# A hybrid attention block on one core: one DMA transpose per pair, an earlier weight load, and another order for the last products

## The chip, the cores and the metric

The kernel runs on one core of a Trainium2 chip. The metric is the device time of the whole program in microseconds, the median of several runs. Beside those runs one execution was recorded by the hardware profiler, and all views of the profile come from it.

## The reference

For a sequence of 2048 positions of width 1024, the block computes

```python
h = rms_norm(x, norm_gain)
qa, ka, va, qb, kb, vb, ga, gb, mg = split(h @ w_in)
# q and k are RMS-normed per head; all softmaxes have a relative-position bias
ya = banded_attention(qa, ka, va, window 128, 8 query heads on 2 kv heads, sink) * silu(ga)
yb = softmax-weighted sum of three dilated attentions, (window, dilation) =
     (128, 1), (512, 4), (2048, 16), 8 heads each, * silu(gb)
merged = sigmoid(mg_a + b) * (ya @ w_branch_a) + sigmoid(mg_b + b) * (yb @ w_branch_b)
out = x + merged @ w_out
```

## The kernel before, in words

**One order for five engines.** The program is written out by a heap of due times. `at(t, f)` puts a step at time t, `until(t)` runs all steps that are due, and every step appends its instructions to the engines' streams. Between engines semaphores hold, within an engine the order of writing. Time is counted in slots. Due times are constants: `W_STEP` for the weights, `Y_PART` and `Y_MAX` for the finished columns of y, `L_LAST` for the last logits, `KQ_BUFS` and `PT_BUFS` for the number of buffers.

**Units and pairs.** The input projection and both attentions go in 14 units of 8 slots each: two A units (two kv heads' worth of the windowed attention, numbers 0 and 2) and twelve B units (two heads of one dilation). In each slot one pair of subsets, 2 × 128 positions, is projected on TensorE (L697, into the bank pj). Matrices are split into a high and a low f16 part, so each product takes three matmuls. ScalarE, VectorE and GpSimd take q, k and v out of the bank, norm and split them into the tile spl, and `Pair.turn` (L781) transposes spl by DMA into kq. A unit's `Item`s, two heads at 128 queries each, come some slots later: logits on PE (L847, bank s), maxima on DVE (L862), exponentials on ACT, the high part p on ACT (L875) and the low part on DVE (L879), a DMA transpose of p into pt (L885), and the product with v on PE (L896, bank pv).

**Queues.** All these DMAs are issued by SyncE in the order of the program: kq (L787), pt (L885), raw weights (`w_load`, L178, two issues of 384 KB at a time), the columns of y and the gates (L946 yo, L977 ytd). An issue that waits for its data holds everything behind it. The raw weights of a unit have one buffer, wraw, free once the unit before has been split; then come four squares on ACT (`w_square`), a sum on PE, and the split. kq has 6 tiles of six 128 × 128 blocks, and B units keep the first one of each residue class in another ring, kq0.

**y.** `YPart` takes finished parts of y: four 128 × 128 transposes on PE (L960, into the one bank pt), a gating on DVE that reads that bank (L967, yo) and a store. After a chunk's fourth part, `max1` to `max3` find the chunk's maximum: ym on DVE, a matmul of ym with ones on PE into the same bank pt (L189), and six small DVE operations on the sum (L196 to L204).

**The last attention slots and stage two.** The last pair's logits are `L_LAST` slots later than the others; PE fills the wait with projections of the merge gates (`mg_step`, L304). Then the branch and output products go in groups of seven products (a scheme of Strassen's kind). `run(g)` writes products 0 to 4 of a group with one or two late ones of the group before between them, and leaves 5 and 6 for the next group. The products share three banks:

```python
PROD = (("A11", 0), ("S1", 2), ("A12", 1), ("S2", 0), ("S4", 2), ("S3", 0), ("A22", 0))
```

The number is the bank of the product. A product adds onto what its bank holds (L1921 for a branch, L1993 for the output), and after each DVE or ACT reads the bank: for the output `put` (L2000) adds it, scaled, to a tile xr, which is stored (L2003) when both of its parts are in. `Out(7)` is the last group of the kernel.

Of the kernel before, what the change touches and what calls it, by code (L numbers as in the profile page):

```python
# [22 lines left out]
F16 = mybir.dt.float16  # L23
I32 = mybir.dt.int32
AF = mybir.ActivationFunctionType
OP = mybir.AluOpType
# [6 lines left out]
NT = S // 128  # L33
# [35 lines left out]
Y_PART = (-0.02, 0.571, 0.797, 0.981, 1.031)  # L69
GATE = (-0.062, 0.084, 0.255)  # L70
W_STEP = (0.1, 0.6, 1.9, 0.445, 4.186, 0.117, 0.301)
W_MAX = (3.542, 3.596)
G_PREP = (5.907,)
N_PREP = (5.948, 6.756, 7.277)
Y_MAX = (0.02, 0.445, 0.485)
S_AT = ((26, 8), (50.5, 5.5), (56, 5.5), (72.5, 5.5), (78, 5.5), (94.5, 4.5), (99, 4.5), (103.5, 4.5))
F_AT = (4.6, .12, 5.0, .33, .16, 7.4)
G_US = dict(look=.25, late=.12, add=.7, hi=.64, dma=.4, wl=7.0, sq=.82, pow=1.5, wh=.72, lo=.76, th=.82, p1=.73, st=3.0,
# [1 line left out]
SEQ = ((1, 0), (1, 1), (8, 0), (8, 1), (2, 0), (2, 1), (9, 0), (9, 1), (3, 0), (3, 1), (10, 0), (10, 1), (4, 0), (4, 1),  # L80
       (5, 0), (5, 1), (6, 0), (6, 1), (7, 0))
G_T0, G_LD, G_SQ = 5.0, 3.0, 2.0
W_RAW, L_LAST = 14.0, 0.3
STD, W_EARLY, G_TH, G_SI, G_CP, K_AT = 5.2, 24.0, 2.0, 4.0, 1.0, (4, 17)
Y_S = 4.0
Y_1 = (.2, .9, 1.6), (13.0, 14.0, 1.6)
# [12 lines left out]
X_US = dict(look=0.25, land=4.3, next=1.45, late=.12, sq=1.14, st=.17, ln=.2, nw=.75, sc=1.24, tr=.8, hi=.5, lo=.62, gs=2.1, pw=1.3,  # L99
            gh=1.06, gl=1.26, mm=.217, th=.6, gt=.63, us=.83, uh=.75, ul=.82, ag=1.0, tl=1.3)  # L100
XT_BUFS = 14
KQ_BUFS = 6
VT_BUFS = 10
PT_BUFS = 4
N_BIAS_A = 384
# [3 lines left out]
def block_kernel(tc, x, w_units, w_gate, w_mrg, w_out, w_bra, w_brk, gain, qkg, sink, bias_a, bias_b, b_merge, out):  # L109
    nc = tc.nc  # L110
    V = nc.vector
    A = nc.scalar
    G = nc.gpsimd
    T = nc.tensor
# [12 lines left out]
    def ucol():  # L127

        ucount[0] += 1
        return ubuf[:, ucount[0] - 1:ucount[0]]  # L130
# [252 lines left out]
    def at(t, f, *args):  # L383
        seq[0] += 1
        heapq.heappush(heap, (t, seq[0], f, args))

    now = [0.0]

    def until(t):
        while heap and heap[0][0] <= t:  # L390
            now[0], _, f, args = heapq.heappop(heap)
            f(*args)

    def chain(steps):

        steps = sorted(steps, key=lambda e: e[0])
        done = [0]

        def go(k):
            if done[0] < k or steps[k][1](*steps[k][2:]) is False:  # L400
                at(now[0] + .04, go, k)
            else:
                done[0] = k + 1

        for k, e in enumerate(steps):
            at(e[0], go, k)
# [107 lines left out]
    class Order:  # L514
# [17 lines left out]
        def run(self):  # L532
            while self.steps:
                best = {}
                for n, s in self.steps.items():
                    t = self.start(n)
                    if t is not None:
                        best.setdefault(s[0], []).append((t, s[3], n))
                eng, c = min(best.items(), key=lambda e: min(e[1])[0])
                t0 = min(c)[0]  # L540
                t, _, n = min((x for x in c if x[0] <= t0 + (0 if eng == "T" else X_US["look"])), key=lambda x: x[1])
                eng, us, _, _, f, args, _ = self.steps.pop(n)
                self.end[n] = self.free[eng] = t + us
                at(t, f, *args)
# [15 lines left out]
    for t in range(NT):  # L560
        g = groups[t]
# [8 lines left out]
        for h in range(2):  # L570
            k = 2 * t + h
# [15 lines left out]
    steps = {}  # L587
# [36 lines left out]
    wk = main.enter_context(tc.tile_pool(name="wk", bufs=2, reuse_waits="tile"))  # L624
# [55 lines left out]
    class Pair:  # L680
# [98 lines left out]
                G.tensor_copy(sp[:, i, nh:, :, :], sp[:, i, nq:nh, ::-1, :])  # L779

        def turn(self):  # L781
            for i, s in enumerate(self.subsets):
                if self.un.shift and s[1] == 0:
                    kq = wk.tile([128, 6, 128], F16, name="kq0", bufs=3)
                else:
                    kq = wk.tile([128, 6, 128], F16, name="kq", bufs=KQ_BUFS)
                nc.sync.dma_start_transpose(out=kq[:], in_=self.sp[:, i].rearrange("p a b c -> p (a b c)"))  # L787
                self.un.kq[s] = kq


    class Item:
# [143 lines left out]
    class YPart:  # L935
# [12 lines left out]
        def plan(self, t):  # L948
            steps = [(t + d, f) for d, f in zip(Y_PART, (self.load, self.turn, self.gate, self.top, self.store))]
            if self.q == 3 and self.chunk < 2:  # L950
                steps += [(t + Y_PART[3] + d, f) for d, f in zip(Y_MAX, (self.max1, self.max2, self.max3))]
            chain(steps)
# [253 lines left out]
    w_forms(NU + SEQ[0][0], 8 * NU)  # L1206
    for u in range(NU + 1):
        t = 8 * u
        steps = [(t + W_STEP[i], w_load, u + 1, (2 * i, 2 * i + 1)) for i in range(2)]
        for i in range(4):  # L1210
            steps.append((t + W_STEP[2] + W_STEP[3] * i, w_square, u + 1, i))
            if u < NU:
                steps += [(t + W_STEP[4] + W_STEP[3] * i, w_hi, u + 1, i),
                          (t + W_STEP[4] + W_STEP[5] + W_STEP[3] * i, w_lo, u + 1, i)]
        chain(steps + [(t + d, f, u + 1) for d, f in zip(W_MAX, (w_sum, w_pow))])

    for k in range(8):
        u = 3 + k
        t = 8 * u
# [10 lines left out]
    t = 0  # L1230
    while t < NPAIR or heap or any(k >= t for k in fill):
        u, j = divmod(t, 8)
        steps = [(f, args) for f, *args in fill.pop(t, [])]
# [70 lines left out]
    def bank():  # L1304
        return ps_p.tile([128, 512], F32, name="fps")

    (sb, ib), (so, io) = (scales[k] for k in "bo")
    ysg, yig, msc, bnd, i_o = (ucol() for _ in range(5))
# [420 lines left out]
    for k in range(2):  # L1729
        g = LAST - 2 + k  # L1730
# [36 lines left out]
    def y_build(s, k, b, b0=None):  # L1767
        load, sums, hi, lo = y_parts(s, k)
        at(b if b0 is None else b0, load)
        for n in range(4):  # L1770
            at(b + Y_S + .4 * n, sums, n)
        for n in range(7):
            at(b + Y_S + .9 + .7 * n, hi, n)
            at(b + Y_S + 1.7 + .7 * n, lo, n)
# [25 lines left out]
    ahead = [y_parts(1, k) for k in range(2)]  # L1800
# [14 lines left out]
    class Seven:  # L1815
# [8 lines left out]
        def after(self, i):  # L1824
            b, r = self.b, self.r
            if i == 0:
                self.copy(0, b[0])
            elif i == 1:
                self.copy(2, b[2])
            elif i == 2:  # L1830
                self.sum(0, b[1])
            elif i == 3:
                self.copy(1, b[0])
            elif i == 4:
                self.sum(1, b[2])
            elif i == 5:
                self.sum(2, b[0])
            else:
                self.last(b[0])
# [16 lines left out]
    def emit(g, i):  # L1856
        until(pos[0])
        mm = g.mm(i)
        us = g.mm_us
        for k, m in enumerate(mm):  # L1860
            until(pos[0] + us * k / len(mm))
            m()
        pos[0] += us
        until(pos[0])
        now[0] = pos[0]
        g.after(i)

    pending = []

    def late():  # L1870
        if pending:
            emit(*pending.pop(0))

    def run(g):
        emit(g, 0)
        if g.n == 1:
            late()
            return
        emit(g, 1)
        late()  # L1880
        emit(g, 2)
        emit(g, 3)
        late()
        emit(g, 4)
        pending.extend(((g, 5), (g, 6)))

    def flush():
        while pending:
            pos[0] += .3
            late()  # L1890
# [5 lines left out]
    WO = rp.tile([128, 7, 2, 4, 512], F16, name="WO")  # L1896
# [78 lines left out]
    class Out(Seven):  # L1975
# [11 lines left out]
        def matmuls(self, i, ps, fresh):  # L1987
            m = mf[self.s, i]
            out = []
            for p in range(4):  # L1990
                for ml, wl in ((0, 0), (0, 1), (1, 0)):
                    k = len(out)
                    out.append(lambda p=p, ml=ml, wl=wl, k=k: T.matmul(  # L1993
                        ps[:], lhsT=m[:, ml, p, :], rhs=WO[:, i, wl, p, :],
                        start=(fresh and k == 0), stop=(k == 11), skip_group_check=True))
            return out

        def put(self, h, n, b, store=False):
            t = self.x[h, n]
            at(now[0] + .2, lambda: V.scalar_tensor_tensor(t[:], b[:], i_o[:], t[:], OP.mult, OP.add))  # L2000
            if store:
                t0 = 128 * self.s + 1024 * h
                at(now[0] + 1.0, lambda: nc.sync.dma_start(  # L2003
                    out=out[t0:t0 + 128, 512 * n:512 * n + 512], in_=t[:]))

        def after(self, i):
            b = self.b
            for h, n, k, store in (((0, 0, 0, False),), ((1, 1, 2, False),), ((0, 0, 1, True),), ((0, 1, 0, False),),
                                   ((0, 1, 2, True),), ((1, 1, 0, True),), ((1, 0, 0, True),))[i]:
                self.put(h, n, b[k], store)  # L2010
# [3 lines left out]
    outs = [Out(s) for s in range(8)]  # L2014

    def AB(s):
        p = pos[0]
        at(p + (4.0 if s else 1.0), g_tiles, s, 1)
        if s == 0:
            at(p + 9, g_tiles, 1, 0)  # L2020
            for i in range(7):
                at(p + WO_AT[0] + WO_AT[1] * i, wo_load, i)
        run(Branch(s, 0))
        run(Branch(s, 1))

    AB(0)
    at(pos[0] + 9, outs[0].load, ((0, 0), (1, 1), (0, 1), (1, 0)))
    AB(1)
    for s in range(8):
        p = pos[0]  # L2030
        if s < 6:
            at(p + .1, g_tiles, s + 2, 0)
            y_build(s + 2, 0, p + 5.0, p + .05)
            y_build(s + 2, 1, p + 14.0)
        if s < 7:
            at(p + (24.0 if s < 6 else 2.0), outs[s + 1].load, ((0, 0), (1, 1)))
            at(p + (31.0 if s < 6 else 15.5), outs[s + 1].load, ((0, 1),))
            at(p + (31.1 if s < 6 else 28.0), outs[s + 1].load, ((1, 0),))
        if s == 6:
            flush()  # L2040
        run(outs[s])
        if s < 6:
            AB(s + 2)
    flush()
# [78 lines left out]
```

## Time and profile before

| | us |
|---|---|
| median of 3 runs | 1914.71 |
| the runs | 1913.5 to 1917.62 |
| the profiled execution, its own time | 1916.55 |
| span of its instructions | 1914.3 |
| PE busy | 1873.9 (98%) |
| DVE busy | 1500.7 (78%) |
| ACT busy | 1250.4 (65%) |
| transposes by DMA of spl into kq | 224 issues |
| transposes by DMA of p into pt | 256 issues |

Times in the views run from the start of the span. A wait is put down to what came last by the profile. The DMA share is that of the core's 16 DMA engines, and a value over 1 means that transfers lay over one another.

### The profile page before, as it was taken

To read this page: it belongs to the slowest core of one execution; us is meant where nothing else is said; L and a number is where in the kernel's file an instruction comes from. 1 tells how busy PE (TensorE), PEld (TensorE's weight loads), DVE (VectorE), ACT (ScalarE), POOL (GpSimd) and SP (SyncE) were. 2 spreads that over 40 slices of the span, in tenths; PEclk is the share of its full clock that TensorE was granted. 3 is DMA by queue.
4 is the path that set the end of the run, shared out by engine and by line. 5 is a ranking of instruction groups with operands and counts; after the bars stand their busy time and mean duration, and the time that the engine had idled before them with its cause. 6 is when DMAs were issued, how large, how long until landed. Compare 5 with 4: busy or idle time off the path is not lost.

```text
span 1914.3 us, 51103 instructions
## 1 busy us (share of the span) xinstructions
PE 1873.9 (98%) x19242; PEld 1438.9 (75%) x19242; DVE 1500.7 (78%) x3835; ACT 1250.4 (65%) x3015; POOL 579.0 (30%) x1363
## 2 busy tenths in 40 slices
PE   6999999999999999999999999999999999999998
PEld 4567887889999899998999899544444446776774
DVE  7679878986887879878788888748679644987885
ACT  8577768887676777777776766565666865433431
POOL 1034343443454435534455444300000001322121
PEclk9999999999999999999999999999999999999999
DMA  6259998988889679888897777786666648854541
GB/s 256 83 98 197 164 185 134 192 161 178 149 161 181 134 158 200 151 170 169 143 179 144 147 154 132 165 309 172 211 198 188 190 156 273 290 164 122 148 148 65
DMA packets 639351, 326.21 MB, mean 170 GB/s; under 512 B 459264, under 2 KB 589952, under 8 KB 636672
## 3 DMA queue, kind: packets, MB, share of 16 engines
q1 hardware_dynamic: 638960, 322.70, 73.3%
q8 instruction: 150, 2.46, 0.6%
q14 instruction: 97, 0.79, 0.2%
q10 hardware_dynamic: 144, 0.26, 0.0%
HBM read 139.08 MB, written 73.66 MB: 111 GB/s over the span
## 4 chain that ended last, share of the span: by engine, by line
PE 90%; DMA 5%; DVE 2%; ACT 1%; issue 1%; POOL 0%; SPq 0%; DVEq 0%; POOLq 0%
PE pj L697 43%; PE fps L1602 17%; PE fps L1921 8%; PE fps L1993 8%; PE s L847 5%; PE pv L896 4%; DMA pt<-p 2%; PE pj L352 2%; PE pj L304 1%; PE fps L304 1%; DMA kq<-spl 1%; PE pt L960 1%; DMA bigl<-sd 1%; DVE pr L862 0%; PE s L482 0%
## 5 line engine op out<-in xcount | busy, mean ns | idle before, releaser
L697 PE MATMUL pj<-wl,XH 128*128 128x128 f16 (+2 forms) x2816 | 715.8, 268 | 0.0
L697 PE MATMUL pj<-wh,XL 128*128 128x128 f16 (+2 forms) x2816 | 712.2, 269 | 0.0
L697 PE MATMUL pj<-wh,XH 128*128 128x128 f16 (+2 forms) x2816 | 709.4, 268 | 0.0
L697 PEld LDWEIGHTS <-XH 128*128 128x128 f16 x5632 | 575.3, 112 | 54.5
L697 PEld LDWEIGHTS <-XL 128*128 128x128 f16 x2816 | 315.9, 112 | 24.0
L862 DVE CUSTOM_DVE_ANT_0 pr<-s,b,ubuf 128x256 f32<-128x256 f32 (+3 forms) x512 | 218.9, 465 | 44.1 <-PE s L847 41.7
L879 DVE SCALAR_TENSOR_TENSOR p<-pr,p 128x512 f16<-128x512 f32 (+2 forms) x256 | 195.7, 765 | 51.6 <-ACT p L875 50.4
L764 POOL TENSOR_TENSOR rw<-rw,g 128x128 f32<-128x128 f32 (+1 forms) x224 | 149.1, 686 | 202.5 <-DVE rw L757 183.2
L1931 POOL TENSOR_TENSOR g<-g,t 128x512 f32<-128x512 f32 x32 | 48.8, 1526 | 523.7 <-DVE t L1854 523.7
L1602 PEld LDWEIGHTS <-wh 128*128 128x128 f16 x1064 | 104.1, 99 | 123.5 <-issue 0.4
L715 ACT ACTIVATE rw<-pj 128x256 f32<-128x256 f32 (+1 forms) x224 | 87.5, 390 | 134.5 <-PE pj L697 134.0
L779 POOL COPY spl<-spl 128x256 f16<-128x256 f16 (+1 forms) x224 | 96.4, 460 | 246.5 <-DVE spl L774 246.5
L875 ACT ACTIVATE p<-pr 128x512 f16<-128x512 f32 (+2 forms) x256 | 157.7, 616 | 14.4 <-DMA pt<-p 10.1
L1921 PE MATMUL fps<-y,bigh 128*128 128x128 f16 x1792 | 153.5, 219 | 0.8 <-DVE r L1854 0.8
L847 PE MATMUL s<-kq 128*128 128x128 f16 (+1 forms) x1856 | 148.2, 218 | 4.8 <-DMA kq<-spl 3.9
L1921 PE MATMUL fps<-y,bigl 128*128 128x128 f16 x896 | 151.7, 219 | 0.0
L1993 PE MATMUL fps<-WO,mf 128*128 128x512 f16 x672 | 150.3, 379 | 0.8 <-DVE xr L2000 0.8
L847 PEld LDWEIGHTS <-kq 128*128 128x128 f16 x2016 | 131.0, 98 | 21.1 <-issue 5.7
L1921 PEld LDWEIGHTS <-bigh 128*128 128x128 f16 x1792 | 139.0, 98 | 8.2 <-issue 0.9
L896 PE MATMUL pv<-vt,pt 128*128 128x65 f16 (+1 forms) x2784 | 132.1, 193 | 8.7 <-DMA pt<-p 7.7
L896 PEld LDWEIGHTS <-pt 128*128 128x128 f16 x3024 | 119.6, 98 | 24.6 <-DMA pt<-p 12.5
L770 ACT ACTIVATE spl<-rw 128x512 f16<-128x512 f32 (+1 forms) x112 | 72.1, 643 | 79.7 <-POOL vt L726 71.4
(252 smaller groups left out, 3815.0 us busy)
## 6 DMA issues: line engine op xcount, KB each, us to landing
wraw<-in_w_units_dram SPq DMA_DIRECT2D x56, 384.0 KB, 4.8
g<-mgd SPq DMA_DIRECT2D x64, 256.0 KB, 5.4
wraw<-in_w_mrg_dram SPq DMA_DIRECT2D x45, 256.0 KB, 4.2
mgd<-t SPq DMA_DIRECT2D x43, 256.0 KB, 2.9
zd<-z SPq DMA_DIRECT2D x128, 66.0 KB, 2.0
zz<-zd SPq DMA_DIRECT2D x64, 132.0 KB, 3.5
xt<-in_x_dram SPq DMA_DIRECT2D x16, 512.0 KB, 7.8
ytd<-yo SPq DMA_DIRECT2D x32, 256.0 KB, 3.5
```

What stands on the lines that cost most here:

```text
L697: out.append(lambda lhs=lhs, rhs=rhs, ch=ch, a=a, b=b, k=k: T.matmul(ps[:, a:b], lhsT=lhs[:, ch, :], rhs=rhs[:, ch, a:b], start=(k == 0), ...
L715: A.activation(self.rw[:, n * i:n * i + n], self.ps[i][:, :n], AF.Copy)
L764: G.tensor_tensor(q[:, i, :un.nq, :], q[:, i, :un.nq, :], g, OP.mult)
L779: G.tensor_copy(sp[:, i, nh:, :, :], sp[:, i, nq:nh, ::-1, :])
L847: T.matmul(self.sv[j][:, o:o + k1 - k0], lhsT=q[:, h, :], rhs=kt[:, un.nq + kh + v * un.nk, k0:k1], start=(v == 0), stop=(v == 1))
L862: V.tensor_tensor_reduce(out=self.pv[:, j, self.p0:self.p0 + W], in0=self.sv[j], in1=un.bias[:, self.h0 + j, self.b0:self.b0 + W], scale=I ...
L875: A.activation(self.sp[:, :128 * n], self.pr, AF.Copy, scale=PSC)
L879: V.scalar_tensor_tensor(self.sp[:, 128 * n:], self.pr, PSC, self.sp[:, :128 * n], OP.mult, OP.subtract)
L896: T.matmul(self.po[:, j, :w], lhsT=p[:, n * j + s, :], rhs=un.v[key][:, vh, c0:c0 + w], start=(k == 0 and s == 0), stop=(k == 2 and s == n ...
L1602: T.matmul(b[k][:], lhsT=w[:, i, ch, :], rhs=xform(PROD[i][0], lo, ch, q), start=(i < 3 and n == 0), stop=(n == 11), skip_group_check=True)
L1921: out.append(lambda p=p, c=c, wl=wl, yl=yl, n=n: T.matmul(ps[:, 128 * p:128 * p + 128], lhsT=w[wl][:, i, c, p, :], rhs=y[:, yl, c, :], sta ...
L1993: out.append(lambda p=p, ml=ml, wl=wl, k=k: T.matmul(ps[:], lhsT=m[:, ml, p, :], rhs=WO[:, i, wl, p, :], start=(fresh and k == 0), stop=(k ...
```

## The change

1. `Pair.turn`: in A units one DMA transpose takes both subsets of a pair (twelve blocks); B units still take two, into the halves of one tile. kq has 4 tiles of twelve blocks; kq0 has one, for dilation 1 alone.
2. `W_SOON`: the raw weights of unit 2 are loaded 1.9 slots sooner and squared 0.5 slot sooner.
3. `Y_MAX`: the matmul of ym and the operations on its sum come 0.065 slot sooner.
4. `L_LAST`: the last pair's logits come 0.1 slot later.
5. The last group on each side (`Branch(7, 1)` and `Out(7)`) takes products in the order 0, 1, 3, 2, 5, 4, 6. `Out(7)` makes its last product in two halves of 256 columns. The right half goes into a bank of its own, and VectorE adds it and stores it while the left half runs; the left half follows, and the output's last tile is stored as two pieces of 128 × 256.

```diff
+W_SOON = (1.9, .5)
-Y_MAX = (0.02, 0.445, 0.485)
+Y_MAX = (0.02, 0.38, 0.42)
-W_RAW, L_LAST = 14.0, 0.3
+W_RAW, L_LAST = 14.0, 0.4
-KQ_BUFS = 6
+KQ_BUFS = 4
...
         def turn(self):
+            kq = wk.tile([128, 12, 128], F16, name="kq", bufs=KQ_BUFS)
+            outs = [kq[:, 6 * i:6 * i + 6] for i in range(2)]
+            if self.un.shift and self.un.n == NT and self.subsets[0][1] == 0:
+                outs[0] = wk.tile([128, 6, 128], F16, name="kq0", bufs=1)[:]
+            if self.un.kind == "A":
+                nc.sync.dma_start_transpose(out=kq[:], in_=self.sp[:].rearrange("p s a b c -> p (s a b c)"))
             for i, s in enumerate(self.subsets):
-                if self.un.shift and s[1] == 0:
-                    kq = wk.tile([128, 6, 128], F16, name="kq0", bufs=3)
-                else:
-                    kq = wk.tile([128, 6, 128], F16, name="kq", bufs=KQ_BUFS)
-                nc.sync.dma_start_transpose(out=kq[:], in_=self.sp[:, i].rearrange("p a b c -> p (a b c)"))
-                self.un.kq[s] = kq
+                if self.un.kind == "B":
+                    nc.sync.dma_start_transpose(out=outs[i], in_=self.sp[:, i].rearrange("p a b c -> p (a b c)"))
+                self.un.kq[s] = outs[i]
...
-        steps = [(t + W_STEP[i], w_load, u + 1, (2 * i, 2 * i + 1)) for i in range(2)]
+        ahead = W_SOON if u == 1 else (0.0, 0.0)
+        steps = [(t + W_STEP[i] - ahead[0], w_load, u + 1, (2 * i, 2 * i + 1)) for i in range(2)]
         for i in range(4):
-            steps.append((t + W_STEP[2] + W_STEP[3] * i, w_square, u + 1, i))
+            steps.append((t + W_STEP[2] + W_STEP[3] * i - ahead[1], w_square, u + 1, i))
...
-    def run(g):
+    def run(g, final=False):
...
-        emit(g, 2)
-        emit(g, 3)
+        for i in (3, 2) if final else (2, 3):
+            emit(g, i)
         late()
-        emit(g, 4)
-        pending.extend(((g, 5), (g, 6)))
+        for i in (5, 4) if final else (4,):
+            emit(g, i)
+        pending.extend(((g, 6),) if final else ((g, 5), (g, 6)))
...
         def matmuls(self, i, ps, fresh):
+            if (self.s, i) == (7, 6):
+                fb = bank()
+                for h in range(2):
+                    c, o = slice(256 - 256 * h, 512 - 256 * h), (fb[:, :256], ps[:, :256])[h]
+                    for p in range(4):
+                        for ml, wl in ((0, 0), (0, 1), (1, 0)):
+                            k = len(out)
+                            out.append(lambda p=p, ml=ml, wl=wl, c=c, o=o, h=h, k=k: T.matmul(
+                                o, lhsT=m[:, ml, p, :], rhs=WO[:, i, wl, p, c], start=(k == 0), stop=(k % 12 == 11),
+                                skip_group_check=True))
+                    if h == 0:
+                        out.append(lambda: self.half(1, fb[:, :256]))
+                return out
...
+        def half(self, j, b, store=True):
+            c, t0 = slice(256 * j, 256 * j + 256), 128 * self.s + 1024
+            t = self.x[1, 0]
+            V.scalar_tensor_tensor(t[:, c], b, i_o[:], t[:, c], OP.mult, OP.add)
+            if store:
+                nc.sync.dma_start(out=out[t0:t0 + 128, c], in_=t[:, c])
...
         def after(self, i):
+            if (self.s, i) == (7, 6):
+                self.half(0, b[0][:, :256])
+                return
+            if (self.s, i) == (7, 5):
+                at(now[0] + .4, lambda: self.half(1, b[0][:, 256:], False))
...
-        run(Branch(s, 1))
+        run(Branch(s, 1), s == 7)
...
-        run(outs[s])
+        run(outs[s], s == 7)
```

Two places show how the rows move. SyncE's queue before, in the second half of the first A unit (spl is a pair's normed q and k, p the probabilities of an item, wraw the raw weights, yo a gate's columns):

```order
L885 DMA_TRANSPOSE pt_1762<-p_1722 128x12x128
L787 DMA_TRANSPOSE kq<-spl 128x6x128 x2
L885 DMA_TRANSPOSE pt_1844<-p_1795 128x12x128
L885 DMA_TRANSPOSE pt_1909<-p_1868 128x12x128
L885 DMA_TRANSPOSE pt_1975<-p_1935 128x12x128
L885 DMA_TRANSPOSE pt_2040<-p_2000 128x12x128
L787 DMA_TRANSPOSE kq<-spl 128x6x128 x2
L885 DMA_TRANSPOSE pt_2115<-p_2073 128x12x128
L946 DMA yo<-gtd_87 128x512
L885 DMA_TRANSPOSE pt_2179<-p_2139 128x12x128
L885 DMA_TRANSPOSE pt_2241<-p_2207 128x12x128
L671 DMA b_2297<-in_bias_b_dram 128x512
```

Behind these rows stand, in the same queue before:

```order
L885 DMA_TRANSPOSE pt_2317<-p_2266 128x12x128
L178 DMA wraw<-in_w_units_dram 128x768 x2
L787 DMA_TRANSPOSE kq<-spl 128x6x128 x2
L946 DMA yo<-gtd_88 128x512
L885 DMA_TRANSPOSE pt_2417<-p_2357 128x12x128
```

The same place of the queue now (lines past the change are one to four higher):

```order
L889 DMA_TRANSPOSE pt_1754<-p_1714 128x12x128
L179 DMA wraw<-in_w_units_dram 128x768 x2
L788 DMA_TRANSPOSE kq<-spl 128x12x128
L889 DMA_TRANSPOSE pt_1837<-p_1787 128x12x128
L889 DMA_TRANSPOSE pt_1902<-p_1861 128x12x128
L179 DMA wraw<-in_w_units_dram 128x768 x2
L889 DMA_TRANSPOSE pt_1970<-p_1928 128x12x128
L889 DMA_TRANSPOSE pt_2035<-p_1995 128x12x128
L788 DMA_TRANSPOSE kq<-spl 128x12x128
L889 DMA_TRANSPOSE pt_2108<-p_2068 128x12x128
L950 DMA yo<-gtd_87 128x512
L889 DMA_TRANSPOSE pt_2172<-p_2132 128x12x128
```

Each pair's two kq transposes have become one, and the loads of wraw have moved from ahead of the kq with yo_88 behind it to two kq sooner.

The second place is PE where the first chunk's maximum is summed, in the B unit behind (pj is the projection's bank, ya a finished part of y, ym the maximum). Before, ahead of the eight matmuls of a pair of logits:

```order
L697 MATMUL pj<-wh,XL 128x256
L697 LDWEIGHTS XH
L697 MATMUL pj<-wh,XH 128x256
L697 LDWEIGHTS XH
L697 MATMUL pj<-wl,XH 128x256
L960 MATMUL pt<-idf,ya 128x128 x4
L697 LDWEIGHTS XL
L697 MATMUL pj<-wh,XL 128x256
L847 LDWEIGHTS kq
```

There is no matmul of ym there; it stands some 30 matmuls further on, behind other projections. Now the same place reads:

```order
L698 MATMUL pj<-wh,XL 128x256
L190 MATMUL pt<-ym,ones 128x1
L698 LDWEIGHTS XH
L698 MATMUL pj<-wh,XH 128x256
L698 LDWEIGHTS XH
L698 MATMUL pj<-wl,XH 128x256
L698 LDWEIGHTS XL
L698 MATMUL pj<-wh,XL 128x256
L851 LDWEIGHTS kq
```

The matmul of ym has come ahead of the four transposes, which now stand behind those eight logits and three more projections; both write the bank pt.

## The prediction

> **What bounds the kernel now.** The page comes first: its totals and the chain that ended last.
>
> ```profile
> span 1914.3 us, 51103 instructions
> PE 1873.9 (98%) x19242; PEld 1438.9 (75%) x19242; DVE 1500.7 (78%) x3835; ACT 1250.4 (65%) x3015; POOL 579.0 (30%) x1363
> PE 90%; DMA 5%; DVE 2%; ACT 1%; issue 1%; POOL 0%; SPq 0%; DVEq 0%; POOLq 0%
> ```
>
> TensorE is busy for 98% of the span and is 90% of the chain. The change takes no matmul columns away, so only the idle stretches of PE and its clock can give time. The second view is the windows by stage: first A unit's start, its end, the B unit behind it, and the middle of the second A unit. The last two rows are from a finer cut, over a stretch of 3.5 us and the one behind it.
>
> ```profile
> core 0: us, PE busy (x) PEld busy (x) DVE busy (x) ACT busy (x) POOL busy (x), PEclk, DMA share, GB/s
> 130.00:160.00 30.00, 28.50 (x376) 20.78 (x372) 28.94 (x71) 25.87 (x60) 13.85 (x27) 1.00 0.93 157
> 160.00:205.00 45.00, 40.13 (x617) 36.76 (x615) 39.27 (x99) 34.43 (x78) 14.95 (x35) 0.97 1.11 207
> 205.00:265.00 60.00, 58.09 (x866) 57.50 (x865) 50.49 (x140) 40.63 (x110) 23.54 (x60) 1.00 0.91 161
> 340.00:400.00 60.00, 58.42 (x759) 49.66 (x757) 54.98 (x142) 51.20 (x120) 25.20 (x49) 1.00 1.04 192
> ...
> 201.90:205.40 3.50, 3.50 (x32) 2.84 (x33) 1.97 (x5) 3.13 (x7) 0.00 (x0) 0.51 1.00 216
> 205.40:210.00 4.60, 4.60 (x81) 4.57 (x80) 3.59 (x9) 2.71 (x9) 0.08 (x1) 1.00 0.97 205
> ```
>
> From 160 to 205 PE lacks 4.9 us, the DMA engines have no room (a share of 1.11), and for 3.5 us right behind that the granted clock is 0.51. What PE waited for, from 82 to 265, then from 300 to 400, in the drain of the attention around 1210, and in the last 55 us (line, releaser: total us, times, longest):
>
> ```profile
> PE pv L896 <- DMA pt<-p: 5.5, 5, 2.0
> PE pt L189 <- DVE yo L967: 0.9, 1, 0.9
> ...
> PE pv L896 <- DMA pt<-p: 2.2, 4, 0.7
> ...
> PE s L847 <- DMA kq<-spl: 1.6, 1, 1.6
> ...
> PE fps L1993 <- DVE xr L2000: 0.8, 1, 0.8
> PE fps L1921 <- DVE r L1854: 0.8, 1, 0.8
> ```
>
> These five places, 11.8 us, are what the change touches, and with the clock they bound what it can bring.
>
> **Where the transposes of p wait.** Three of the five products that waited, in the timeline of PE, then the DVE operation that makes the second one's p, and SyncE's queue around its transpose:
>
> ```profile
> 154.21 0.71 PE L896 MATMUL pv<-vt,pt 128*128 128x65 f16 x18 [0.67 <-DMA pt<-p]
> 182.42 0.71 PE L896 MATMUL pv<-vt,pt 128*128 128x65 f16 x18 [1.91 <-DMA pt<-p]
> 201.89 1.15 PE L896 MATMUL pv<-vt,pt 128*128 128x65 f16 x18 [2.03 <-DMA pt<-p]
> ...
> 171.40 0.96 DVE L879 SCALAR_TENSOR_TENSOR p<-pr,p 128x768 f16<-128x768 f32 x1 [0.19 <-ACT p L875]
> ...
> 171.44 1.41 SPq L178 DMA_DIRECT2D wraw<-in_w_units_dram  x2
> 172.94 2.67 SPq L787 DMA_TRANSPOSE kq<-spl  x2
> 175.66 0.57 SPq L946 DMA_DIRECT2D yo<-gtd  x1
> 176.34 1.43 SPq L885 DMA_TRANSPOSE pt<-p  x1
> ...
> L885 SPq DMA_TRANSPOSE pt<-p x13: 1425/2530/3185, 156.8 to 200.1; - x13
> DMA to landing us min/median/max: 3.7/5.0/6.7
> ...
> L787 SPq DMA_TRANSPOSE kq<-spl x28: 1209/1239/2356, 99.1 to 259.3; - x28
> ...
> L178 SPq DMA_DIRECT2D wraw<-in_w_units_dram x4: 423/500/924, 171.4 to 182.5; - x4
> ```
>
> p is there at 172.36 (171.40 + 0.96), its transpose is issued only at 176.34: SP has in between two loads of raw weights, two transposes of kq and a load of yo to issue. So 4.0 us pass before the issue and 6.0 behind it (to 182.4), where the quickest of the thirteen landed after 3.7.
>
> **Part 1, one transpose of 12 blocks for a pair.** Only A units change, 16 of 112 pairs. Two issues of 1.239 (the median) become one; the nearest rows of a 12-block transpose are those of pt, whose issue takes 1.425 at best and 3.185 at worst. Per pair SP then gains 2.48 − 1.43 = 1.05 us or loses 0.71. I take the gain at the places where the queue is late only because SP is, since those waits lie after a stretch of issues without pause. The bytes stay the same, so DMA time is left alone. What the 6-block form hid was that its first half could land sooner; the matmuls of L847 need the second subset as well, so nothing waits for a half alone.
>
> **Part 2, the second A unit's raw weights 1.9 slots sooner.** Two pairs of loads leave the places ahead of the kq at 172.94 (1.41 us of SP there) and, a little later, ahead of another pt. By the order they go two kq sooner: one pair of loads ahead of a kq, the other between the second and third of the four transposes of p behind it. There SP had slack:
>
> ```profile
> SPq L885 <- DVE p L879: 4.7, 4, 1.7
> ```
>
> This is the queue's own wait from 136 to 158: 4.7 us in which SP stood ready for p. Four loads at the 0.5 us of the row above go into that, and DMA share there was 0.93 against 1.11 later. The squares come half a slot sooner on ACT, the same four operations, ahead of ACT's exps; ACT is at 25.87 of 30 there, so I cost them at nothing, with one exp (the wait of 1.7 above as the most) as the price if that cover is gone.
>
> Together, parts 1 and 2 take 1.05 + 1.41 = 2.46 us of the 4.0 before the issue at 176.34, and take the load's DMA traffic out of the crowded window. Of the five waits (5.5 us) four lie there or behind, 4.8 us; the one that ends at 154.2 lies where the loads now go, and I keep its 0.7. Of the four I keep 1.8, some 0.45 each, since DVE (39.27 of 45 busy) would make p late in part: 4.8 − 1.8 = **3.0** us, with bounds of 0 and 5.5. The window at 0.51 lasts 3.5 us and does 1.75 us of work at full clock: **1.7** us come back if the wait of 2.03 that ends at 201.89, where the slow stretch begins, is gone.
>
> On that clock the row says that a wait of 2.0 us, in 11.9 us with 9.5 busy, was followed by the slow stretch. [...]
>
> In the second A unit part 1 acts alone (its weights went with the first). Four waits, 2.2 us, the longest 0.7, each shorter than the 1.05 that SP gains per pair; but DVE is at 54.98 of 60, so p itself is late at some: **1.3** of 2.2, bounds 0 and 2.2.
>
> **Part 3, y's maximum.** ym stood ready long before the bank was free, and PE's first matmul of L189 waited for L967 to read the bank that four transposes had filled:
>
> ```profile
> 252.88 0.16 DVE L983 TENSOR_TENSOR ym<-ym 128x1 f32<-128x1 f32 x1
> ...
> 257.97 0.67 DVE yo L967
> 258.63 0.14 issue
> 258.77 0.35 PE pt L189 x2
> ```
>
> ym is made at 253.04. Put ahead of the transposes at 255.2, that matmul finds an empty bank. What is late next is the transposes, which must wait until DVE's L196 has read the sum; they stand eight logits and more matmuls behind it in the new order, a microsecond or more. I take **0.9**, bounds 0 and 0.9; a wait of the transposes as long as the old one is the lower bound.
>
> **Part 4, last logits 0.1 slot later.** Three matmuls of the filling (L304) move ahead of them.
>
> ```profile
> 1204.86 5.25 DMA kq<-spl
> ...
> 1226.33 2.59 PE pj L304 x12
> ```
>
> 2.59 / 12 = 0.216 each, so 3 × 0.216 = **0.65** of the 1.6 that PE stands until the kq lands at 1210.1 is filled. The work behind it moves by as much later, but PE has only filling matmuls to do there. Bounds 0 and 1.6.
>
> **Part 5, the last products.** Two products in a row on one bank wait until DVE has read it: 0.8 (L1993) and 0.8 (L1921), both named above; in the new order another bank's product of 2.6 us stands between, against 0.75 us of DVE.
>
> ```profile
> 1907.87 2.75 PE L1993 MATMUL fps<-WO,mf 128*128 128x512 f16 x12 [0.84 <-DVE xr L2000]
> 1910.65 0.75 DVE L2000 SCALAR_TENSOR_TENSOR xr<-fps,ubuf,xr 128x512 f32<-128x512 f32 x1 [2.84 <-PE fps L1993]
> ...
> 249.97 0.55 PE pj L697 x5
> ...
> L1763 DVE SCALAR_TENSOR_TENSOR y<-tq,ubuf,y 128x256 f16<-128x256 f32 x60 | 28.8, 483 | 2.9 <-ACT y L1759 2.9
> ```
>
> The last product becomes 24 matmuls of 256 columns; five of that width took 0.55, so 24 take 2.64 against 2.75: no loss. The DVE operation that closes it is 0.75 at 512 wide and 0.48 at 256 (the row with f16 out), 0.3 less, and the other half's work lies beside the matmuls. 0.8 + 0.8 + 0.3 = **1.9**, bounds 1 and 2.
>
> **The sum.** 3.0 + 1.7 + 0.9 + 1.3 + 0.65 + 1.9 = 9.45 us. The profiled execution took 1916.55 (span 1914.3 and 2.25 around it), 1.84 above the median of three runs, 1914.71 (1913.5 to 1917.62). From the median: 1914.71 − 9.45 = **1905.3**.
>
> **The rivals.**
>
> *All of it goes.* The transposes' waits vanish whole in both A units, the clock stays up, and the drain's wait too: 5.5 + 1.7 + 0.9 + 2.2 + 1.6 + 1.9 = 13.8, which gives 1900.9. For it: SP's lateness explains most of the 4.0 us. Against it: DVE and the DMA share.
>
> *Another engine holds the A units.* If p, or the DMA engines at 1.11 with unchanged bytes, sets the pace, the transposes land as late as now and only parts 3, 4 and 5 count: 0.9 + 0.65 + 1.9 = 3.45, or 1911.3. For it: 54.98 of 60 on DVE; against it: p was ready 4.0 us ahead of its issue.
>
> [...]
>
> *Slower: the big transpose holds the queue.* A 12-block transpose behind another is held for up to 3.185 us in the rows above. If each merged kq is, the following pt is issued 3.185 − 2.48 = 0.71 later than now; over 16 pairs 11.3 us. Parts 3 to 5 still give 3.45: 1914.71 + 11.3 − 3.45 = 1922.6. It decides where the pt behind a kq is issued more than 3.4 us after that kq (176.34 − 172.94 now). Against it: the yo and two waits of the ring lie in that 3.4 already, and only nine of the pairs have PE waiting.
>
> That the change doesn't do what it says holds in part: transposes per pair reach only the A units, so the 96 pairs of B units give nothing; that is in the sum.
>
> **How the numbers follow.** The forecast has 0.45, the full recovery 0.20, the A units held otherwise 0.16, the clock 0.09, the slower case 0.10. The range reaches from a little under the full recovery, 1899, to a little over the third case, 1912, and leaves out the slower case and the edges. About 0.2%, 3.8 us, is what a measurement here can tell from no change, as the three runs lie 4.1 apart. Forecast, full recovery and clock are faster by more: 0.74. The third case is a gain of 3.45, within it: 0.16. Slower: 0.10.
>
> **What would show it.** Right: between 160 and 205 PE's waits for pt near 2.5 us, a granted clock of 1.00 around 202, the pt behind a merged kq issued under 3 us after it; no wait of L189's matmul for L967; the drain's wait for kq near 1.0; no wait for xr or r in the last 50 us. Wrong: an issue of the merged kq near 3 us, a wait for pt around 152 to 160 longer than 0.7, or squares that push exps back there.

## The result and the profile after

The changed kernel takes 1908.05 us in the median of 6 runs (1906.96 to 1910.0) against 1915.3 before (6 runs of the same kind, 1913.5 to 1918.9). The ratio is 0.996, 95% interval 0.9947 to 0.9973: faster by 7.25 us, where the prediction had 9.45. The profiled execution took 1910.0 us, 2.0 above its median, and its span is 1908.0.

The page of the changed kernel, for the rows shown of before:

```profile
span 1908.0 us, 51104 instructions
PE 1873.8 (98%) x19254; PEld 1441.1 (76%) x19254; DVE 1501.3 (79%) x3837; ACT 1250.6 (66%) x3015; POOL 581.7 (30%) x1363
```

PE's busy time is what it was (1873.9 before), so the gain is idle time that has gone. Its windows, with the same cuts, and in the last two rows a finer cut:

```profile
core 0: us, PE busy (x) PEld busy (x) DVE busy (x) ACT busy (x) POOL busy (x), PEclk, DMA share, GB/s
130.00:160.00 30.00, 26.70 (x357) 19.58 (x355) 27.86 (x69) 24.43 (x57) 11.95 (x24) 1.00 0.98 185
160.00:205.00 45.00, 43.04 (x649) 39.95 (x648) 40.22 (x101) 36.55 (x84) 17.55 (x38) 0.96 1.09 189
205.00:265.00 60.00, 59.41 (x883) 59.07 (x881) 52.38 (x152) 41.42 (x108) 24.89 (x62) 1.00 0.96 165
340.00:400.00 60.00, 59.00 (x759) 50.70 (x758) 55.28 (x142) 52.45 (x125) 25.97 (x52) 1.00 1.05 196
...
178.00:184.60 6.60, 4.69 (x67) 4.33 (x64) 6.46 (x18) 3.04 (x6) 3.39 (x4) 1.00 1.19 187
184.60:188.10 3.50, 3.49 (x42) 3.31 (x43) 3.22 (x7) 3.05 (x7) 1.24 (x2) 0.55 1.07 235
```

From 160 to 205 PE is busy for 2.9 us more, but from 130 to 160 for 1.8 less: it was 28.50 there before. The stretch at half clock is still there, at another place: 0.55 over 3.5 us, as 0.51 over 3.5 us before. What PE waited for now, from 82 to 265 (three rows), from 300 to 400, and from 400 to 1195 (where before had 2.3 us in 2 waits):

```profile
PE pv L900 <- DMA pt<-p: 3.6, 3, 1.9
PE s L851 <- DMA kq<-spl: 1.5, 1, 1.5
PE s L851 <- DVE nmA L866: 0.7, 2, 0.5
...
PE pv L900 <- DMA pt<-p: 0.9, 2, 0.6
...
PE s L851 <- DMA kq<-spl: 2.7, 3, 1.1
```

The wait of L189 for L967 (0.9), the drain's wait for kq (1.6) and both of 0.8 at the end have no row any more, nor has the wait of 2.03 at 201.89. A wait for kq that was not there before has come to the first A unit. In the timeline of PE it stands at 153.87:

```profile
153.87 0.61 PE L851 MATMUL s<-kq 128*128 128x128 f16 x8 [1.46 <-DMA kq<-spl]
156.08 0.71 PE L900 MATMUL pv<-vt,pt 128*128 128x65 f16 x18 [1.12 <-DMA pt<-p]
184.61 0.89 PE L900 MATMUL pv<-vt,pt 128*128 128x65 f16 x18 [1.92 <-DMA pt<-p]
```

SyncE's queue of the changed kernel just before the first two of them, and how long that kq took from its issue to landing:

```profile
145.69 1.37 SPq L179 DMA_DIRECT2D wraw<-in_w_units_dram  x2
147.10 2.58 SPq L788 DMA_TRANSPOSE kq<-spl  x1
149.86 5.54 SPq L889 DMA_TRANSPOSE pt<-p  x2
...
DMA to landing us min/median/max: 6.7/6.7/6.7
```

Before, the same pair's two transposes were issued at 145.7 and 147.3 and landed like this:

```profile
L787 SPq DMA_TRANSPOSE kq<-spl x2: 1278/1446/1613, 145.7 to 147.3; - x2
DMA to landing us min/median/max: 2.8/3.0/3.1
```

The issue came no later than the second of these two; it is the landing that took 6.7 us instead of 3. Two things have changed there, the size of the transpose and the two loads of 384 KB ahead of it. Part 1 alone, one of the experiments below, has the merged transpose at this place with no load ahead:

```profile
L787 SPq DMA_TRANSPOSE kq<-spl x1: 1808/1808/1808, 145.7 to 145.7; - x1
DMA to landing us min/median/max: 4.3/4.3/4.3
```

So 1.3 us of the difference go with the size and 2.4 with the loads.

### The profile page after: what moved, and what is told of

It is laid out like the page before. It is cut to its first block, busy times and chain, and to the rows that moved or that the text cites. A ratio compares the mean times of both kernels' runs of the same rounds, so it can differ in the third digit from the quotient of the medians.

```text
span 1908.0 us, 51104 instructions
## 1 busy us (share of the span) xinstructions
PE 1873.8 (98%) x19254; PEld 1441.1 (76%) x19254; DVE 1501.3 (79%) x3837; ACT 1250.6 (66%) x3015; POOL 581.7 (30%) x1363
## 3 DMA queue, kind: packets, MB, share of 16 engines
q8 instruction: 150, 2.46, 0.6%
## 4 chain that ended last, share of the span: by engine, by line
PE 89%; DMA 6%; DVE 2%; ACT 1%; issue 1%; POOL 0%; SPq 0%; DVEq 0%; POOLq 0%
PE pj L698 42%; PE fps L1607 18%; PE fps L1927 8%; PE fps L2012 7%; PE s L851 5%; PE pv L900 4%; DMA kq<-spl 2%; DMA pt<-p 2%; PE pj L353 2%; PE pj L305 1%; PE fps L305 1%; PE pt L964 1%; DMA bigl<-sd 1%; PE s L483 0%; DVE pr L866 0%
## 5 line engine op out<-in xcount | busy, mean ns | idle before, releaser
L851 PE MATMUL s<-kq 128*128 128x128 f16 (+1 forms) x1984 | 152.2, 217 | 5.7 <-DMA kq<-spl 4.2
```

The source lines that it names most:

```text
L851: T.matmul(self.sv[j][:, o:o + k1 - k0], lhsT=q[:, h, :], rhs=kt[:, un.nq + kh + v * un.nk, k0:k1], start=(v == 0), stop=(v == 1))
```

## The experiments

Five parts are told apart: 1, one transpose per pair; 2, the raw weights sooner; 3, y's maximum; 4, the last logits; 5, the last products. Each kernel was timed in five rounds beside the kernel before; ratios are to it.

**Parts 1 and 2 alone, 1 alone, 2 alone, and the other three.** The edits, each on the kernel before:

```diff
 parts 1 and 2:  + turn() with one 12-block transpose in A units, + W_SOON = (1.9, .5)
 part 1:         + turn() with one 12-block transpose in A units (with its ring, KQ_BUFS = 4)
 part 2:         + W_SOON = (1.9, .5)
 parts 3 to 5:   + Y_MAX = (0.02, 0.38, 0.42), + L_LAST = 0.4, + run(g, final), half()
```

> Parts 1 and 2 alone (one 12-block kq transpose per pair in A units, raw weights of unit 2 sooner). Theory of the queue: both parts relieve SyncE in the A units, 1.3 us in the second and 1.7 in the first, so about 3 us less than before, ratio 0.9984; the first A unit keeps waits of about 3.6 us for pt, 1.5 for kq, and its stretch at half clock. Rival (the loads only move a wait): the same total here, but all of it from part 1, which the next two kernels tell.

> Part 1 alone. Theory of the queue: 1.3 us less in the second A unit and about 1 in the first, 2.3 in all, ratio 0.9988; the wait for kq at 154 that the changed kernel has is absent, since no load stands ahead of that kq. Rival (the loads only move a wait): about 3 us less, all that parts 1 and 2 bring.

> Part 2 alone. Theory of the queue: 1 to 2 us less, ratio 0.9993; waits for pt between 180 and 203 fall from 4.9 us to under 3, and a new wait of 1 to 1.5 us stands near 154, for kq or pt. Rival (the loads only move a wait): within 0.5 us of before; what goes from 180 to 203 comes back near 154.

> Parts 3, 4 and 5 alone (y's maximum, last logits, last products). By the waits that are gone in the changed kernel's profile, 0.9 + 1.5 + 1.9 = 4.3 us less than before, ratio 0.9978; by the terms of the prediction, with 0.65 for the last logits, 3.45 less. Rival: the drain's wait for kq went because the A units changed, not by the 0.1 slot; then it stands here still with about 1 us.

| kernel | us | ratio, 95% interval |
|---|---|---|
| parts 1 and 2 | 1912.74 | 0.9987 (0.9978 to 0.9996) |
| part 1 | 1910.18 | 0.9976 (0.9967 to 0.9985) |
| part 2 | 1917.83 | 1.0017 (1.0008 to 1.0026) |
| parts 3 to 5 | 1909.1 | 0.9973 (0.9963 to 0.9984) |

The kernel before took 1914.32 here. Part 1 brings 4.1 us, more than either theory had; part 2 does not move a wait at no cost but loses 3.5, and 2.6 on top of part 1. Both theories were wrong on part 2, and parts 1 and 2 together bring 1.6 us where both had 3. The three others bring 5.2; the drain's wait for kq is 0.6 in their profile, so most of it goes without the change in the A units, against the rival. Waits of PE for DMA in part 1 alone, from 82 to 265 and from 300 to 400, and the issues and landings of its sixteen merged transposes:

```profile
PE pv L899 <- DMA pt<-p: 4.2, 3, 1.9
...
PE pv L899 <- DMA pt<-p: 0.2, 1, 0.2
...
L787 SPq DMA_TRANSPOSE kq<-spl x16: 1424/1519/2584, 99.4 to 371.6; - x16
DMA to landing us min/median/max: 3.6/4.2/5.9
```

No wait for kq stands in the A units. The second A unit loses 0.2 instead of 2.2, and one issue of 1.52 takes the place of two of 1.24, 0.96 less. In part 2 alone the same views read:

```profile
PE pv L897 <- DMA pt<-p: 4.3, 5, 1.5
...
PE pv L897 <- DMA pt<-p: 2.8, 5, 0.8
...
154.00 0.71 PE L897 MATMUL pv<-vt,pt 128*128 128x65 f16 x18 [1.48 <-DMA pt<-p]
167.63 0.71 PE L897 MATMUL pv<-vt,pt 128*128 128x65 f16 x18 [0.60 <-DMA pt<-p]
```

As expected of a wait that moves, 1.48 stands at 154 where 0.67 stood, and 0.60 behind it. From 82 to 265 the sum is still 1.2 less than before, so this stretch doesn't show the 3.5 us that the runs lose; and this execution, 1915.23, was 2.6 us under the median of part 2 alone.

**The change without part 2, and its two single parts.**

```diff
 without part 2: - W_SOON = (1.9, .5)
 part 5 alone, on the kernel before: + run(g, final), half()
 part 4 alone, on the kernel before: + L_LAST = 0.4
```

> The change without part 2 (the raw weights of unit 2 at their old place). Part 1 alone gave 4.1 us, parts 3 to 5 gave 5.2, part 2 lost 3.5. If the parts add up, 9.3 us less than before, about 1905.0, ratio 0.9951, and 2 to 3 us less than the changed kernel: part 2 is a loss. Rival (parts 1 and 2 belong together once the rest is in): about the changed kernel's 1907 to 1908.

> Part 5 alone (the last products). By the prediction 1.9 us less than before, ratio 0.9990, both waits of 0.8 gone and the last DVE operation 0.5 instead of 0.75. Parts 3 to 5 together gave 5.2 where the waits sum to 4.3; if the rest of it comes from here, 2.8 less.

> Part 4 alone (the last pair's logits 0.1 slot later). By the prediction 0.65 us less than before and a wait of about 1.0 for kq left there; by the changed kernel's profile, where no such wait is left, 1.5 less; in the profile of parts 3 to 5 a wait of 0.6 was left, which says 1.0 less.

Without part 2 the kernel takes 1904.31, ratio 0.9943 (0.993 to 0.9955), 9.5 us less than before (1913.77 in this group): the parts add up, 4.1 + 5.2 = 9.3, and its median is the lowest of all that ran. Part 5 alone: 1911.67, ratio 0.9987 (0.9979 to 0.9996), 2.1 less. Part 4 alone: 1912.8, ratio 0.9993 (0.9984 to 1.0002), 1.0 less, which is inside what the runs can tell; its profile has a wait of 0.4 for kq left of the 1.6:

```profile
PE s L847 <- DMA kq<-spl: 0.4, 1, 0.4
```

**What part 2 costs: bytes, issues or squares.** First the changed kernel with an eighth of the bytes in those loads; then with the loads sooner but the squares where they were.

```diff
-            nc.sync.dma_start(out=raw[:, 2 * i:2 * i + 2, :n], in_=src[:, 2 * i:2 * i + 2, :])
+            m = 48 if u == 2 else n
+            if m < n:
+                G.memset(raw[:, 2 * i:2 * i + 2, m:n], 0.5)
+            nc.sync.dma_start(out=raw[:, 2 * i:2 * i + 2, :m], in_=src[:, 2 * i:2 * i + 2, :m])
...
-W_SOON = (1.9, .5)
+W_SOON = (1.9, 0.0)
```

> The changed kernel with the raw weights of unit 2 loaded for 48 of 384 columns; the other columns are a constant from GpSimd, so that unit's weights are left out for the most part. Issues, places and waits on the queue stay as they are, the bytes ahead of the kq fall to an eighth. If the bytes are the price of part 2, the waits for kq and pt between 150 and 160 (1.5 and 1.1 us) fall under 0.5 in sum, and the time is 2 to 3 us under the changed kernel's, about 1905. If it is the issue time on SyncE, the waits stay over 2 us in sum and the time near 1907 to 1908.

> The changed kernel with the loads of unit 2 sooner, but its squares on ScalarE at their old place. If the loads' bytes are what part 2 costs, the time stays within 1 us of the changed kernel's, 1907 to 1908, with the waits of 1.5 for kq and 1.1 for pt near 155. If the squares are, it falls to about 1904.5.

With few bytes: 1905.58, ratio 0.9952 (0.9939 to 0.9966). The kq behind the small loads was issued at 147.2, landed after 3.8, and nothing waited for it:

```profile
L791 SPq DMA_TRANSPOSE kq<-spl x1: 1447/1447/1447, 147.2 to 147.2; - x1
...
DMA to landing us min/median/max: 3.8/3.8/3.8
```

So the bytes are what held the kq, which landed after 6.7 behind the full loads. The expectation held only by half: the pt behind it still waits, 1.67 us, with two issues of loads (1.42) ahead as in the changed kernel. The issues of the loads have a price too, then. With the squares at their old place: 1906.5, ratio 0.9958 (0.9946 to 0.997), against 0.996 of the changed kernel, which the runs don't tell apart. The squares are not the cost. There the kq landed after 5.5, and the wait went to the pt behind it:

```profile
150.68 0.61 PE L851 MATMUL s<-kq 128*128 128x128 f16 x8 [0.22 <-DMA kq<-spl]
154.33 0.71 PE L900 MATMUL pv<-vt,pt 128*128 128x65 f16 x18 [2.56 <-DMA pt<-p]
```

**Other places for the loads, and part 3 alone.** On parts 1, 3, 4 and 5: the four loads one at a time, each behind a transpose of p; and all of them 0.25 slot later than before.

```diff
 one at a time:  + steps = [(t + d, w_load, 2, (i,)) for i, d in enumerate((-1.5, -1.25, -1.02, -.5))]   (u == 1)
 later:          + W_SOON = (-0.25, 0.0)
 part 3 alone:   + Y_MAX = (0.02, 0.38, 0.42)
```

> Parts 1, 3, 4, 5, and the four loads of unit 2's raw weights 1 to 1.6 slots sooner, one at a time, each behind a transpose of p instead of two together ahead of a kq. If the price of part 2 is two loads' bytes ahead of one transpose (a kq or pt that lands 2 us late), then no wait over 1 us stands between 150 and 165, the two waits of 2 us at 182 and 200 shrink, and the time is at or under the 1904.3 of parts 1, 3, 4, 5. If any load in that stretch costs its bytes wherever it stands, the time is 1906 to 1908.

> Parts 1, 3, 4, 5, and the four loads of unit 2's raw weights 0.25 slot later than before instead of sooner, so that two of them stand behind the kq and the transpose of p that PE waits for 2 us at 182. If the bytes ahead of that transpose are what it waits for, that wait falls to about 0.5 and another of 0.5 to 1 may come behind, net 1 to 1.5 us less than parts 1, 3, 4, 5 (1904.3), about 1903. If the transposes wait for each other (12 blocks each, one after another) the time stays at 1904 to 1905.

> Part 3 alone (y's maximum). By the prediction 0.9 us less than before, with the wait of 0.9 for L967 gone. Parts 3 to 5 gave 5.2, part 5 alone 2.1 and part 4 alone 1.0, which leaves 2.1 for this one if the parts add up; ratio 0.9989 to 0.9995, inside what the runs can tell.

One at a time: 1905.08, ratio 0.9949 (0.9936 to 0.9961), no different from the loads at their old place. In the first A unit it does what was expected: the longest wait is 0.9, where parts 1, 3, 4 and 5 with the loads unmoved keep two of 2 us:

```profile
PE pv L900 <- DMA pt<-p: 2.7, 3, 0.9
...
PE pv L899 <- DMA pt<-p: 5.3, 4, 2.0
```

What that wins, 2.6 us, is lost further on in these two profiles, from 400 to 1195, in waits for kq. That row, first of the loads one at a time, then of the loads unmoved:

```profile
PE s L851 <- DMA kq<-spl: 4.2, 5, 1.5
...
PE s L850 <- DMA kq<-spl: 0.5, 2, 0.3
```

Later: 1907.13, ratio 0.9964 (0.9952 to 0.9977), 2 to 3 us worse than unmoved, a miss. The transpose that PE had waited 2.01 us for at 182 now landed in time, 4.4 us after its issue instead of 6.6, as expected if the loads held it. But the next one, now with loads ahead of it, landed after 6.7, and PE waited 1.62 for it and 0.81 for the one behind; 3.2 us of kq waits stand from 400 to 1195. In the first A unit the loads again move a wait. Part 3 alone: 1913.0, ratio 0.9993 (0.9984 to 1.0002), 1.1 less, not told from nothing by the runs; the wait for L967 is gone in its profile. Parts 3, 4 and 5 each alone sum to 4.2 us, against 5.2 together.

Over all profiles, PE's waits for kq from 400 to 1195 are 0.5 to 2.3 us in the seven kernels with the loads at their old place, 1.5 with the small loads, and 2.7 to 4.5 in the six where the full loads moved, sooner or later. Those units are hundreds of microseconds behind the loads, and from 400 to 1195 SyncE issues its DMAs in the same order in all of them. It may be where part 2 loses what the first A unit does not show, but this is argued and not shown: each value is from one execution, and what carries the effect that far was not found.

## Why the prediction was right, and where it was not

The sign and the range were right; one part was read the wrong way round, and that the sum came within 2.2 us is in part luck. The terms of parts 1 and 2 with the clock, 3.0 + 1.3 + 1.7 = 6.0 us, measured 1.6 together, and those of parts 3 to 5, 3.45, measured 5.2: the two errors point opposite ways.

*Part 1* was sized by SyncE's time, 1.05 us a pair; the issues show 0.96, and the second A unit gave 2.0 where 1.3 was taken when part 1 stood alone (1.3 with part 2). The runs give 4.1 for it: in the profiles the waits for pt fall by 1.3 and 2.0 us in the two A units, and a mean granted clock under 1.000 came less often, in 3 of 11 runs against 24 of 30 (below), which at 1.7 us each (3.5 us at 0.51) is an estimated 0.9 us. The rival in which the big transpose holds the queue did not decide the time, as its issue was 1.52 in the median, but its sign shows at one place: the longest issue, 2.58 in part 1 alone and 3.70 in the changed kernel, stands ahead of the transpose of p that PE then waits 1.92 for, in both, as it waited 1.91 before. Part 1 also makes the ring of kq deeper, four pairs instead of three, and no run has that alone. In the profile before, all waits of SyncE ahead of a kq from 82 to 1195, 243.4 us, are put down to GpSimd and none to PE, which frees that ring, so the depth is not what held these issues.

*Part 2* is the step that failed: "Four loads at the 0.5 us of the row above go into that". The slack was SyncE's, and the loads' issues used it only in part without harm, as the wait of 1.67 with few bytes shows. But the DMA engines were at a share of 0.93, and the loads' bytes made the kq behind them land after 6.7 us instead of 4.3. The prediction counted what the loads' bytes would free in the crowded window and not what they would cost ahead of another transfer on which PE waits. Between 160 and 205 the waits for pt fell from 4.9 to 1.9 us, just the 3.0 that were expected; at 154 to 156 the waits for kq and pt rose from 0.7 to 2.6, and a wait of 0.6 for pt stands at 227, near the place at which PE had waited 1.0 for ACT. So from 82 to 265 the waits for transposes are only 0.4 less (5.5 before, 3.6 + 1.5 after). The way to the 3.0 was not the predicted one either. The wait from which it was read stays, 1.92 instead of 1.91, and the three behind it are gone. Of the 4.0 us before the issue at 176.34, 2.46 were to go. The same place of the changed kernel, the DVE operation that makes p and SyncE's queue up to its transpose:

```profile
173.27 0.96 DVE L883 SCALAR_TENSOR_TENSOR p<-pr,p 128x768 f16<-128x768 f32 x1 [0.19 <-ACT p L879]
...
173.88 3.70 SPq L788 DMA_TRANSPOSE kq<-spl  x1
177.62 0.58 SPq L950 DMA_DIRECT2D yo<-gtd  x1
178.31 1.28 SPq L889 DMA_TRANSPOSE pt<-p  x1
```

p is there at 174.23 and its transpose is issued 4.1 us later: no load stands ahead any more, but the issue of the merged kq takes 3.70. With the squares at their old place the delay is 2.0; why it differs was not found.

Three of the prediction's own signs of being wrong are thus there: this issue of 3.70, the pt behind it issued 4.4 us after it and not under 3, and a wait for pt of 1.12 at 156. The signs at L189 and in the last 50 us came out right, the clock around 202 is 1.00, and the drain's wait is gone wholly where 1.0 was said to stay.

*The clock's 1.7 us* did not come in the profile: 0.55 from 184.6 to 188.1, after a wait of 1.92. Over the runs it comes in part. Of the fourteen profiles, five have a mean granted clock of 0.999 and nine have 1.000. From 160 to 205 the five have 0.96 or 0.97, which is what one stretch of 3.5 us at 0.5 makes of 45 us, and the eight of the nine that were read by stage have 1.00. The mean was 1.000 in 4 of the 6 runs of the changed kernel, and in 40 of 55 runs of all kernels with part 1; without part 1 in 39 of 130, 25 of 78 for the kernel before. In the first group the kernel before had it in 6 of 30 runs, with a median of 1913.4, against 1914.94 for the 24 others. It is a matter of how often, not a term that is there or gone. The case named "clock", which had a chance of 0.09, is the one that the profile shows: 9.45 without the 1.7 is 7.75, or 1907.0, nearer to the 1908.05 than the forecast. But that is luck, since the four runs with a mean of 1.000 took 1906.96 to 1908.09 as well. That this stretch goes with the wait ahead of it was the author's estimate from one place of the profile before; what sets it off was not shown.

*Parts 3 and 5* went as said: 0.9 and both 0.8 are gone from the profile. The last operation on DVE is 0.48, and the 24 matmuls of 256 columns take 2.78:

```profile
1901.92 2.78 PE L2003 MATMUL fps<-WO,mf 128*128 128x256 f16 x24
1904.74 0.48 DVE L2028 SCALAR_TENSOR_TENSOR xr<-fps,ubuf,xr 128x256 f32<-128x256 f32 x1 [0.83 <-PE fps L2003]
```

*Part 4* was sized low: it took 1.2 us (part 4 alone) to 1.6 us (the changed kernel) of the wait away in the profiles, not 0.65. The logits that wait and the group of logits before them, first in the kernel before, then in part 4 alone with two rows that stand between:

```profile
1203.37 0.61 PE L847 MATMUL s<-kq 128*128 128x128 f16 x8
...
1208.28 0.28 PE L847 MATMUL s<-kq 128*128 128x128 f16 x2
1210.15 0.49 PE L847 MATMUL s<-kq 128*128 128x128 f16 x6 [1.60 <-DMA kq<-spl]
...
1201.58 0.61 PE L847 MATMUL s<-kq 128*128 128x128 f16 x8
...
1206.71 0.52 PE L896 MATMUL pv<-vt,pt 128*128 128x65 f16 x12
...
1207.50 0.60 PE L960 MATMUL pt<-idf,ya 128*128 128x128 f32 x4
1207.93 0.28 PE L847 MATMUL s<-kq 128*128 128x128 f16 x2
1208.60 0.49 PE L847 MATMUL s<-kq 128*128 128x128 f16 x6 [0.39 <-DMA kq<-spl]
```

From group to group it is 4.91 us before and 6.35 with part 4, 1.44 more. The three filling matmuls are 0.65 of it; a product with v (0.36 until the next row begins) and four transposes of y (0.43) have moved ahead of the logits as well, which the prediction left out.

The sum of 9.45 is by chance that of the change without part 2 (9.5): a loss was taken for a gain. On top of the other parts it is 2.2 us by the gains (7.25 and 9.5) and 3.3 by the ratios (0.996 and 0.9943). The intervals of these two overlap; that of part 2 alone, 1.0008 to 1.0026, lies wholly on the side of a loss.

## What to carry to other kernels

A free moment of the queue that issues was not a free moment of the engines that move the bytes: where SyncE had waited 4.7 us for p, the DMA share was 0.93, and the kq behind the loads landed after 6.7 us instead of 4.3. Before a load is moved, look at which transfer with a waiting consumer lands behind it, and how full the DMA engines are there. Two DMA transposes whose data come together were cheaper as one where the queue was late: an issue of 1.52 us for two of 1.24, and 4.1 us over the whole kernel. A part that looks harmless in a bundle deserves a run without it; here the bundle was 0.4% faster, and one of its five parts, alone, cost 0.17%.

## What the runs showed of the hardware that was not expected

A wait of PE of about 2 us was followed by half clock in some profiles and not in others. In the profile before, the granted clock is 0.51 from 201.9 to 205.4, and the wait of 2.03 ends at 201.89; in the changed kernel it is 0.55 from 184.6 to 188.1, and the wait of 1.92 ends at 184.61. The three other profiles with a mean of 0.999, of parts 3 to 5, part 5 alone and part 4 alone, have a longest wait for pt of 2.4, 2.2 and 2.5 us from 82 to 265. But the change without part 2 has waits of 2.01 and 1.84, and the one with the squares at their old place a wait of 2.56, and in both the clock is 1.00 from 130 to 265 and 1.000 in the mean. From run to run it differs as well: the kernel before had a mean of 1.000 in 25 of 78 runs.

At one place of the queue a 12-block transpose landed after 4.3 us with no load ahead (part 1 alone), 3.8 behind two loads with an eighth of the bytes, and 6.7 behind two loads of 384 KB, though its issue, 1.45 to 2.58 us, differs by little over 1 us.
